# One core, a two-layer decoder trunk: the operand of the compression's first layer written position by position by engines, and fourteen weight pieces split by transfers

## The chip, the core and the metric

The kernel runs on one core of one Trainium2 chip. The core has five engines that run at the same time, each through its own list of instructions in order: TensorE (PE, matrix products; its weight loads are listed as PEld), VectorE (DVE), ScalarE (ACT), GpSimd (POOL) and SyncE (SP, which here only starts transfers). Transfers run on 16 DMA engines that all queues share. The metric is device time in microseconds (us) of one launch; three runs of the kernel before gave 584.83, 585.29 and 585.83 us, median 585.29.

## What is computed

The input is 256 tokens of width 1024, in float32. Layer 0 is a recurrent block (two input products, a convolution of width 4, gates, a scan, an output product) and a squared-ReLU MLP of width 4096. Layer 1 is sparse attention and a second MLP. The attention has 16 heads in four groups and three branches. The change lies in the first branch, which compresses keys and values:

```python
def _compress(z, pe, w1, w2):
    B, S, G, DH = z.shape                       # 1, 256, 4, 64
    n_chunk = S // CMP_STRIDE                   # 16
    nc = n_chunk - CMP_RATIO + 1                # 15
    chunks = z.reshape(B, n_chunk, CMP_STRIDE, G, DH)
    blocks = jnp.concatenate([chunks[:, r:r + nc] for r in range(CMP_RATIO)], axis=2)
    blocks = blocks + pe[None, None, :, None, :]
    flat = jnp.transpose(blocks, (0, 1, 3, 2, 4)).reshape(B, nc, G, CMP_LEN * DH)
    return jax.nn.gelu(flat @ w1, approximate=True) @ w2
```

So 15 overlapping blocks of 32 positions, for four groups, each of 32 x 64 numbers, go through a product with `w1` (2048 to 64), a gelu and a product with `w2`. This is done for keys and for values. `flat @ w1` is the first layer that the title speaks of.

## The kernel before

**Precision and pieces.** All large products are made from a high and a low part in the fast float32 format ("fp32r"): three products for one (lines 328, 329, 330 in `mm3`). A weight is stored as pieces of 128 x 1024 numbers, 512 KB, in the order in which they are used. A piece is brought to the array in one of two ways. Split by engines: SP loads it into one of five `raw` buffers (L274), ACT or DVE casts it to the high part in one of seven `whl` buffers (L288 or L336), DVE subtracts (L297 or L333) to get the low part. Split by transfers (`split_dma`): a transfer from POOL's queue loads it straight into the high buffer (L388, the target's type does the rounding), ACT or DVE writes the negated high part into the low buffer (L390), and a second transfer from POOL's queue adds the piece to that (L392). `BY_DMA` names the pieces that go the second way; before, these are eight of the fifteen pieces from q3 on.

**Stages.** By the trace PE's last product of layer 0's recurrent block starts at 89.6 us and layer 0's MLP ends at 263.8; the attention section's products run from there to 398.7, and the second MLP and the final norm end the program. In the MLPs the order is written out by hand. In the two other sections a planner (`Plan`) sets it: each operation is added with its engine or a choice of engines, an assumed duration, what it reads and writes, and a due time; random shifts from a list of seeds move the due times; a list schedule gives the start of each, and instructions are emitted in that order. Another list of seeds gives another order. Real waits are by semaphores, so the planned times only set the order on each engine.

**The attention section.** First come eight projections named by `EARLY` (ks0 kw0 q0 q1 ck0 ck1 cv0 cv1), then q2, the values (`v`, five pieces, L1019 to L1021), then q3, ks1, kw1 and q4 to q7 as fillers between the attention of the heads, and the output projection in two halves (o00 to o03, o10 to o13). Each head has its scores (L1149, L1150), a masked minimum on DVE (L1156), an exponential on ACT (L1159), a rescale on ACT or DVE (L1178), transposes on PE into banks 5 and 6 (L1189), copies of these as high part on ACT (L1192) and low part on DVE (L1193), and the product with the values (L1214, L1216).

**The compression.** `cproj` makes the projections ck and cv (two chunks each); after each, DVE multiplies by the norm (L943) into a buffer `tt` of 128 x 256. Four transfers of 64 x 240 numbers from SP's queue (L364, by `move`) then bring it into `zf`, the first layer's operand in the tile `zwoh`; there are sixteen in all. `zf` has 122 columns z (61 for keys and 61 for values: four groups of 15 blocks and one column of position codes) and 16 positions l in a block. `hidden` makes sixteen plain float32 matmuls (L957), one a position, 128 x 122 each: `e.matmul(hp(), w1[:, l], zf[:, :, l], ...)`. The planner takes 0.9 us for four of them. Before, the 16 positions of a column are neighbours in memory, so the 122 columns that one matmul reads lie 64 bytes apart. The two columns of position codes come by two small transfers from DRAM (L931). Behind `hidden` stands a chain of small operations: L963 (ACT, two copies), L965, L967, L968 (DVE), L969 (ACT), L970 and L971 (DVE), then the second layer on PE (L978 for keys, L997 for values).

Of the kernel before, what the change touches and what calls it, by code (L numbers as in the profile page):

```python
# [28 lines left out]
NB = 15  # L29
# [4 lines left out]
LATE = "q2 v q3 ks1 kw1 q4 q5 q6 q7".split()  # L34
TE = 2.73
W1T, T1, TH, TC, T2, T3, THS, THD, THT, NEARLY = -3.89, 3.12, 0.0, 4.6, 4.94, 3.03, 13.46, 6.73, 5.46, 8
SEEDS, ROUNDS, SHIFT, MOVES, SPREAD = ((3,), (144, 22097, 77409, 21939, 78114, 80006, 60630, 7069, 62773, 82469, 25830, 79801, 92020, 84794, 19920, 86923, 46302, 34626)), 6, 1.5, 12, 3.0
HPEN, LPEN, APEN, LEAD = 0.56, 1.0, 0.0, 9.0
RPEN = 0.51
WARM = 16  # L40
BY_DMA, DLEAD, NPEN = "q3 kw1 q5 q7 o01 o03 o11 o13", 8.0, 0.3
MLAG = (3.4, 4.0)
PLACED = "ks0 kw0 q0 q1 q2".split()
NI, NFINE = 3, 3
# [43 lines left out]
class Plan:  # L88
# [8 lines left out]
    def add(self, eng, dur, fn=None, r=(), w=(), t=0.0, lag=None):  # L97

        if fn is None:
            eng, fn = eng, dur  # L100
        if isinstance(eng, str):
            eng = [(eng, dur, 0.0)]
        i, deps = len(self.tasks), set()
        for k in r:
            if k in self.writer:
                deps.add(self.writer[k])
            self.readers.setdefault(k, []).append(i)
        for k in w:
            deps.update(self.readers.pop(k, ()))
            if k in self.writer:  # L110
                deps.add(self.writer[k])
            self.writer[k] = i
        deps.discard(i)
        self.tasks.append((eng, fn, sorted(deps), t, lag))
# [124 lines left out]
def trunk_kernel(ctx: ExitStack, tc: tile.TileContext, x_in, vec_in, const_in, w2_in, wts, out):  # L239
    nc = tc.nc  # L240
    ctx.enter_context(tc.manual_schedule())
    pe, dve, act, pool = nc.tensor, nc.vector, nc.scalar, nc.gpsimd
# [92 lines left out]
    def copy(o, a):  # L335
        return lambda e: (e.copy if e is act else e.tensor_copy)(o, a)  # L336

    zcols = lambda x: x[:, :S]
    HI = [("act", 0.31, 0.0), ("dve", 0.21, APEN)]
# [139 lines left out]
    vec = consts.tile([P, V_N], F32, name="vec")  # L479
# [55 lines left out]
    with ExitStack() as ph:  # L535
        rg = ph.enter_context(tc.tile_pool(name="rg", bufs=1))
        sec = Section()
        add, table = sec.add, sec.table
# [18 lines left out]
        for x in FIRST.split():  # L557
            n = 1 + x.endswith("+")
# [18 lines left out]
        for k in range(KC):  # L577
            g = vec[:, V_GM + k:V_GM + k + 1]
            t = 0.6 * k - 3
# [240 lines left out]
    with ExitStack() as ph:  # L820
# [96 lines left out]

        pre = ph.enter_context(tc.tile_pool(name="ct", bufs=1))
        ZW = 61
        zf = zw[0][:, :2 * ZW * 16].rearrange("p (z l) -> p z l", l=16)  # L920
        w1 = zw[1].rearrange("p (l c) -> p l c", l=16)
        zok, wok = [("oh", j) for j in range(8)], [("ol", j) for j in range(8)]
        cb = pre.tile([P, 1], F32, name="cb")
# [4 lines left out]
        bd = osumt.rearrange("p a (j e) -> p a j e", j=4)  # L928
        for i in range(2):
            pecol = (V_PEK, V_PEV)[i]  # L930
            add("sp", 0.5, lambda e, i=i, c=pecol: e.dma_start(zf[:, ZW * i + 60], vec_in[:, c:c + 16]), r=zok,  # L931
                w=[("z", i, "p")], t=W1T, lag=2.0)
            o, ws = offs[-1] + 4 * P * 1024, slice(8 * i, 8 * i + 8)
            add("sp", 1.5, lambda e, o=o, ws=ws: e.dma_start(w1[:, ws], wts[o:o + P * 2048].rearrange(
                "(p l c) -> p l c", p=P, l=16)[:, ws]), w=wok[4 * i:4 * i + 4] + ["loads"], t=W1T, lag=2.0)
        add("pool", 0.15, lambda e: e.memset(hid, 0.0), w=["hid"], t=-5)

        def cproj(i, gp, b, t, step):
            z, zk = proj_t(("ck", "cv")[i], gp, b, t, step)
            t += 4 * step  # L940
            n = ti["n"] = ti["n"] + 1
            x, xk = tt[n % 3], ("tt", n % 3)
            add("dve", 0.34, lambda e: e.tensor_tensor(x, z(), rs, op=OP.mult), r=[zk, "rs"], w=[xk], t=t)  # L943
            for hf in range(2):
                g = gp * 2 + hf
                for j in range(2):
                    dst = zf[own_(j), ZW * i + g * NB:ZW * i + (g + 1) * NB].rearrange("p n l -> p (n l)")
                    sec.move(dst, x[own_(hf), j * 16:j * 16 + 240], [xk] + zok, [("z", i, g, j)], t + 0.5, "sp")

        def hidden(b, t):  # L950
            hp = zview("hp", b, lambda x: x[:, :2 * ZW])
# [489 lines left out]
```

## Time and profile before

| what | number |
|---|---|
| median of three runs | 585.29 us (584.83 to 585.83) |
| the profiled execution | 585.05 us, its span 583.3 us |
| PE busy | 569.1 us, 98% of the span |
| PEld busy | 558.6 us, 96% |
| DVE busy | 418.3 us, 72% |
| ACT busy | 354.6 us, 61% |
| POOL busy | 56.3 us, 10% |
| DMA | 108.39 MB, 186 GB/s over the span |

Times in the trace count from the span's start. A PE row's duration runs from its start to its modelled end, and rows overlap; how fast PE really goes is read from start to start. "Idle before" names what ended an engine's wait. A row of 16 plain float32 matmuls of the program appears as 32 rows in the trace, two passes each. Line numbers of the changed kernel are one higher than before from line 947 on (L957 becomes L958, L1159 becomes L1160).

### The profile page before, as it was taken

The numbers are of one execution on the slowest core, as the hardware profiler recorded it, in microseconds if no ns is written. First come the engines' busy times: TensorE is split into PE (matmuls) and PEld (weight loads), VectorE is DVE, ScalarE is ACT, GpSimd is POOL, SyncE is SP. The second block draws the span as 40 slices with busy tenths as digits, with TensorE's granted clock in tenths as the row PEclk, the third lists the DMA queues.
The fourth block names the chain that finished last, engine by engine and source line by source line (L and its number), as shares of the span: only waits on it lengthen the run. The fifth ranks groups of instructions, "written<-read, shape, count | busy, mean of one in ns | idle before, by whom it ended". The sixth has DMA issues, their size and how long they took to land.

```text
span 583.3 us, 12179 instructions
## 1 busy us (share of the span) xinstructions
PE 569.1 (98%) x4756; PEld 558.6 (96%) x4756; DVE 418.3 (72%) x862; ACT 354.6 (61%) x712; POOL 56.3 (10%) x69
## 2 busy tenths in 40 slices
PE   8999999999999999999999989999999999999994
PEld 7999999999999999999999988989999999999994
DVE  6999998767665645647749989999866766464432
ACT  7699674856654433437628999986865664343410
POOL 1200000000000112211011100000000000132320
PEclk8999999999999999999999999999999999999998
DMA  8943575656556565566496776433666767467402
GB/s 286 389 127 136 182 229 197 222 188 199 195 186 213 184 217 177 189 222 217 107 332 173 157 185 172 140 70 109 227 212 183 199 198 241 156 185 219 139 2 72
DMA packets 34617, 108.39 MB, mean 186 GB/s; under 512 B 4576, under 2 KB 8304, under 8 KB 34560
## 3 DMA queue, kind: packets, MB, share of 16 engines
q1 hardware_dynamic: 31632, 98.61, 51.6%
q0 software_dynamic: 2352, 8.49, 6.5%
q8 instruction: 37, 0.61, 0.4%
q10 hardware_dynamic: 576, 0.53, 0.3%
q14 instruction: 20, 0.16, 0.1%
HBM read 103.48 MB, written 1.05 MB: 179 GB/s over the span
## 4 chain that ended last, share of the span: by engine, by line
PE 88%; ACT 5%; DVE 4%; DMA 1%; issue 0%; SPq 0%; DVEq 0%; ACTq 0%
PE bank L328 27%; PE bank L329 26%; PE bank L330 26%; PE bank L690 2%; ACT pt L1159 2%; PE bank L957 1%; ACT pt L1178 1%; DMA raw<-in_dram 1%; PE bank L1189 1%; DVE ptl L1193 1%; PE bank L1019 1%; ACT pth L1192 1%; PE bank L1021 1%; PE bank L1020 1%; DVE pt L1156 1%
## 5 line engine op out<-in xcount | busy, mean ns | idle before, releaser
L328 PE MATMUL bank<-hhl,whl 128*128 128x256 f32 x768 | 215.2, 280 | 1.5 <-DVE whl L336 1.2
L330 PE MATMUL bank<-hhl,whl 128*128 128x256 f32 x768 | 213.3, 278 | 0.2 <-DVE whl L333 0.2
L329 PE MATMUL bank<-hhl,whl 128*128 128x256 f32 x768 | 212.9, 277 | 0.0
L297 DVE TENSOR_TENSOR whl<-raw,whl 128x1024 fp32r<-128x1024 f32 x118 | 147.5, 1272 | 2.7 <-ACT whl L288 2.7
L328 PEld LDWEIGHTS bank<-hhl,whl 128*128 128x128 f32 x768 | 144.8, 189 | 2.4 <-ACT whl L336 1.4
L330 PEld LDWEIGHTS bank<-hhl,whl 128*128 128x128 f32 x768 | 144.7, 188 | 0.7 <-DVE whl L333 0.6
L329 PEld LDWEIGHTS bank<-hhl,whl 128*128 128x128 f32 x768 | 144.9, 189 | 0.2
L328 PE MATMUL bank<-uhl,whl 128*128 128x256 f32 x512 | 141.4, 276 | 0.0
L330 PE MATMUL bank<-uhl,whl 128*128 128x256 f32 x512 | 141.3, 276 | 0.0
L329 PE MATMUL bank<-uhl,whl 128*128 128x256 f32 x512 | 141.3, 276 | 0.0
L288 ACT CAST whl<-raw 128x1024 fp32r<-128x1024 f32 x119 | 121.3, 1043 | 23.0 <-issue 18.8
L328 PEld LDWEIGHTS bank<-uhl,whl 128*128 128x128 f32 x512 | 96.1, 188 | 0.0
L329 PEld LDWEIGHTS bank<-uhl,whl 128*128 128x128 f32 x512 | 96.1, 188 | 0.0
L330 PEld LDWEIGHTS bank<-uhl,whl 128*128 128x128 f32 x512 | 96.1, 188 | 0.0
L532 DVE TENSOR_TENSOR xt<-xt,bank 128x256 f32<-128x256 f32 x40 | 16.1, 418 | 84.4 <-PE bank L330 84.4
L333 DVE TENSOR_TENSOR whl<-raw,whl 128x1024 fp32r<-128x1024 f32 (+3 forms) x64 | 66.5, 1060 | 5.3 <-ACT whl L336 5.2
L785 ACT ACTIVATE u<-t 128x256 f32<-128x256 f32 x64 | 26.7, 417 | 56.1 <-DVE t L780 55.5
L336 ACT CAST whl<-raw 128x1024 fp32r<-128x1024 f32 (+3 forms) x54 | 50.4, 952 | 14.1 <-DMA raw<-in_dram 9.4
L780 DVE SCALAR_TENSOR_TENSOR t<-bank,rstd 128x256 f32<-128x256 f32 x64 | 26.9, 423 | 42.9 <-PE bank L330 42.4
L1317 ACT ACTIVATE xg<-xt,vec 128x256 f32<-128x256 f32 x8 | 4.1, 510 | 47.9 <-DVE xt L532 47.9
L1159 ACT ACTIVATE pt<-pt,mx 128x256 f32<-128x256 f32 (+1 forms) x64 | 28.6, 448 | 3.4 <-DVE mx L1156 3.3
L502 POOL TENSOR_TENSOR acc<-xt 128x256 f32<-128x256 f32 x2 | 3.0, 1521 | 266.0 <-DVE xt L532 266.0
(207 smaller groups left out, 822.8 us busy)
## 6 DMA issues: line engine op xcount, KB each, us to landing
raw<-in_dram SPq DMA_DIRECT2D x167, 512.0 KB, 4.0
whl<-in_dram POOLq DMA_DIRECT2D x16, 512.0 KB, 5.8
gw<-in_dram SPq DMA_DIRECT2D x4, 512.0 KB, 8.4
raw<-in_dram SPq DMA_DIRECT2D x6, 256.0 KB, 5.6
xt<-in_dram SPq DMA_DIRECT2D x4, 256.0 KB, 5.5
zwol<-in_dram SPq DMA_DIRECT2D x2, 512.0 KB, 5.5
zwoh<-tt SPq DMA_DIRECT2D x16, 60.0 KB, 2.7
raw<-in_dram SPq DMA_DIRECT2D x2, 456.0 KB, 5.3
```

The lines of the kernel that those rows point to most:

```text
L288: (act.copy if eng is None else eng.tensor_copy)(hi_t[i % NSPL][:, :n], raw_t[i % NRAW][:, :n])
L297: (eng or dve).tensor_tensor(lo[:, :n], raw_t[i % NRAW][:, :n], hi[:, :n].bitcast(F32), op=OP.subtract)
L328: pe.matmul(ps, wh, xh, start=start, stop=False)
L329: pe.matmul(ps, wh, xl, start=False, stop=False)
L330: pe.matmul(ps, wl, xh, start=False, stop=stop)
L333: return lambda e: e.tensor_tensor(o, a, h.bitcast(F32), op=OP.subtract)
L336: return lambda e: (e.copy if e is act else e.tensor_copy)(o, a)
L532: dve.tensor_tensor(xt[:, m], xt[:, m], z, op=OP.add)
L690: e.matmul(z(), gw[b][:, o:o + P], xb[2 * b + k], start=k == 0, stop=k == 1)
L780: dve.scalar_tensor_tensor(t, z, 0.0, rs, op0=OP.max, op1=OP.mult)
L785: act.activation(u, t, AF.Square)
L1159: add("act", (0.39, 0.49)[qc], lambda e, row=row, j=j: e.activation(row, row, AF.Exp, bias=mx[:, j:j + 1], scale=-1.0, accum_out=sm[:, j:j ...
```

## The change

`zf` is laid out position by position: the 122 columns of one position are neighbours, the 16 positions of a column lie 488 bytes apart. The sixteen transfers are replaced by sixteen copies of 64 x 240 numbers on ACT or DVE (`HI`, a choice that the planner makes), and the two small transfers by two POOL copies from `vec`, which is in SBUF since the program's start. `BY_DMA` holds fourteen pieces: q4, q6, o00, o02, o10 and o12 are added, so that from q3 on only ks1 is split by engines. And the seeds are others, so the planner's order of the attention section is another. The matmuls, their number and their shapes stay. The sections before and after keep their order.

```diff
@@ -34,11 +34,11 @@
-SEEDS, ROUNDS, SHIFT, MOVES, SPREAD = ((3,), (144, 22097, 77409, ..., 34626)), 6, 1.5, 12, 3.0
+SEEDS, ROUNDS, SHIFT, MOVES, SPREAD = ((3,), (123, 87858, 62944, ..., 89816)), 6, 1.5, 12, 3.0
...
-BY_DMA, DLEAD, NPEN = "q3 kw1 q5 q7 o01 o03 o11 o13", 8.0, 0.3
+BY_DMA, DLEAD, NPEN = "q3 q4 kw1 q5 q6 q7 o00 o01 o02 o03 o10 o11 o12 o13", 8.0, 0.3
@@ -917,7 +917,7 @@
-        zf = zw[0][:, :2 * ZW * 16].rearrange("p (z l) -> p z l", l=16)
+        zf = zw[0][:, :2 * ZW * 16].rearrange("p (l z) -> p z l", l=16)
@@ -928,8 +928,8 @@
         for i in range(2):
             pecol = (V_PEK, V_PEV)[i]
-            add("sp", 0.5, lambda e, i=i, c=pecol: e.dma_start(zf[:, ZW * i + 60], vec_in[:, c:c + 16]), r=zok,
-                w=[("z", i, "p")], t=W1T, lag=2.0)
+            add("pool", 0.15, lambda e, i=i, c=pecol: e.tensor_copy(zf[:, ZW * i + 60], vec[:, c:c + 16]), r=zok + ["vec"],
+                w=[("z", i, "p")], t=-5)
@@ -944,8 +944,9 @@
                 for j in range(2):
-                    dst = zf[own_(j), ZW * i + g * NB:ZW * i + (g + 1) * NB].rearrange("p n l -> p (n l)")
-                    sec.move(dst, x[own_(hf), j * 16:j * 16 + 240], [xk] + zok, [("z", i, g, j)], t + 0.5, "sp")
+                    dst = zf[own_(j), ZW * i + g * NB:ZW * i + (g + 1) * NB]
+                    y = x[own_(hf), j * 16:j * 16 + 240].rearrange("p (n l) -> p n l", l=16)
+                    add(HI, copy(dst, y), r=[xk] + zok, w=[("z", i, g, j)], t=t + 0.5)
```

How the order moves is shown at three places. First PE at the first layer of the compression. Before, where `whl,hhl` with 304 columns are the values:

```order
L1020 MATMUL bank_3612<-whl,hhl 128x304
L1021 MATMUL bank_3612<-whl,hhl 128x304
L957 MATMUL bank_3641<-zwoh,zwol 128x122 x16
L1019 MATMUL bank_3612<-whl,hhl 128x304
L1020 MATMUL bank_3612<-whl,hhl 128x304
```

Now, where bank_3557 is the projection q2:

```order
L329 MATMUL bank_3557<-hhl,whl 128x256
L330 MATMUL bank_3557<-hhl,whl 128x256
L958 MATMUL bank_3578<-zwoh,zwol 128x122 x16
L328 MATMUL bank_3557<-hhl,whl 128x256
L329 MATMUL bank_3557<-hhl,whl 128x256
```

The sixteen matmuls stood behind thirty matmuls of the values and now stand inside q2, before all of the values. Between the last matmul of cv1 and them stand 16 others (2 + 6 + 2 + 6: scores, q2, scores, q2).

Second DVE and ACT at the same place in the changed kernel. On DVE `tt_3215` and `tt_3216` are the two chunks of cv, and `zwoh` is the operand:

```order
L943 TENSOR_TENSOR tt_3215<-bank_3479,rstd 128x256
L336 COPY zwoh<-tt_3215 64x15x16 x3
L1157 ISA pt,mx_3238<-bank_3533,cst 128x256
L1157 ISA mx_3238 128x1
L1157 ISA pt,mx_3238<-bank_3533,cst 128x256
L1157 ISA mx_3238 128x1
L943 TENSOR_TENSOR tt_3216<-bank_3514,rstd 128x256
L336 COPY zwoh<-tt_3216 64x15x16 x3
```

On ACT, from the last copy to the gelu's part of the chain:

```order
L336 CAST whl<-raw_79 128x1024
L1160 ACTIVATE pt,sm_3242<-pt,mx_3238 128x256 x2
L336 COPY zwoh<-tt_3216 64x15x16
L1160 ACTIVATE pt,sm_3242<-pt,mx_3238 128x128 x2
L1160 ACTIVATE pt,sm_3243<-pt,mx_3239 128x128
L964 COPY cb<-bank_3578 64x1 x2
L390 ACTIVATE whl<-whl 128x1024
L970 ACTIVATE gy<-gy 128x60
```

Of the sixteen copies nine are on DVE and seven on ACT, and for the last chunk it is three and one. A negation of a piece that a transfer brings (L390) now stands between L964 and L970 on ACT. In all, DVE has six subtractions L333 of whole pieces fewer, two whole casts L336 fewer, two L390 more, and of the rescales (L1178) six with 256 columns and nine with 128 more, which ACT has fewer; ACT has four whole casts fewer and four L390 more, and four more casts of 64 or 128 x 256 that DVE gives up.

Third POOL's queue, which before had eight L388 and eight L392 and now has fourteen of each; the part behind the memory fills in the changed kernel:

```order
L388 DMA whl<-in_dram 128x1024
L392 DMA whl<-in_dram 128x1024
L388 DMA whl<-in_dram 128x1024 x3
L392 DMA whl<-in_dram 128x1024
L1054 COPY gcm<-gts 128x4x2 x4
L388 DMA whl<-in_dram 128x1024
L392 DMA whl<-in_dram 128x1024 x2
L388 DMA whl<-in_dram 128x1024 x2
L392 DMA whl<-in_dram 128x1024 x3
L388 DMA whl<-in_dram 128x1024 x3
L392 DMA whl<-in_dram 128x1024 x2
```

An L392 waits for the L390 of its piece, and what stands behind it on POOL waits with it. On SP's queue the sixteen moves are gone, and the loads of `raw` that stood behind them follow the loads that stood ahead of them; six loads of `raw` are gone too.

More of the change, by code (lines that the diff above doesn't have):

```diff
@@ L36 @@
 W1T, T1, TH, TC, T2, T3, THS, THD, THT, NEARLY = -3.89, 3.12, 0.0, 4.6, 4.94, 3.03, 13.46, 6.73, 5.46, 8
-SEEDS, ROUNDS, SHIFT, MOVES, SPREAD = ((3,), (144, 22097, 77409, 21939, 78114, 80006, 60630, 7069, 62773, 82469, 25830, 79801, 92020, 84794, 19920, 86923, 46302, 34626)), 6, 1.5, 12, 3.0
+SEEDS, ROUNDS, SHIFT, MOVES, SPREAD = ((3,), (123, 87858, 62944, 72224, 13667, 58707, 28766, 10748, 461, 68576, 75909, 30898, 22973, 69747, 33127, 16225, 86495, 85454, 50293, 89816)), 6, 1.5, 12, 3.0
 HPEN, LPEN, APEN, LEAD = 0.56, 1.0, 0.0, 9.0
```

## The prediction

> **What bounds the kernel now.** I read the page's busy times first, then the table of 40 slices, then windows of the attention section, then the waits of PE, and last single rows around the first layer of the compression. From the page's two first parts:
>
> ```profile
> PE 569.1 (98%) x4756; PEld 558.6 (96%) x4756; DVE 418.3 (72%) x862; ACT 354.6 (61%) x712; POOL 56.3 (10%) x69
> PE   8999999999999999999999989999999999999994
> DVE  6999998767665645647749989999866766464432
> ACT  7699674856654433437628999986865664343410
> PEclk8999999999999999999999999999999999999998
> ```
>
> PE is the bound nearly everywhere. The slices in which DVE and ACT are as full as PE are those of the attention section. Time can come from two sources there: PE work that gets shorter, and PE waits that go. The clock is full, so no time comes from it. Both MLPs and layer 0 keep their instructions and their order; I give them no term.
>
> The attention section by windows (busy of PE, PEld, DVE, ACT, POOL with instructions, then clock, DMA share, GB/s):
>
> ```profile
> 262.00:310.00 48.00, 47.68 (x372) 47.06 (x372) 32.77 (x84) 24.87 (x58) 6.26 (x13) 1.00 0.73 224
> 310.00:400.00 90.00, 86.74 (x659) 80.24 (x659) 84.98 (x320) 84.69 (x255) 8.01 (x11) 1.00 0.56 140
> PE bank L1189 <- DVE ptl L1193: 1.9, 2, 1.5
> PE bank L1189 <- ACT osum L1225: 0.4, 1, 0.4
> ```
>
> Up to 310 us DVE and ACT have 15 and 23 us to spare and PE waits 0.3 us. From 310 to 400 us all three are at 94% or more; PE idles 90 - 86.74 = 3.3 us, and the named waits are for DVE and ACT. Some waiting doesn't show as idle, because a row of PE lasts longer than its share:
>
> ```profile
> 360.59 0.39 PE L328 MATMUL bank<-oh,whl 128*128 128x256 f32 x1
> 361.05 0.39 PE L329 MATMUL bank<-ol,whl 128*128 128x256 f32 x1
> 361.28 0.28 PE L330 MATMUL bank<-oh,whl 128*128 128x256 f32 x1
> 306.03 0.28 PE L1020 MATMUL bank<-whl,hhl 128*128 128x256 f32 x1
> 306.15 0.28 PE L1021 MATMUL bank<-whl,hhl 128*128 128x256 f32 x1
> 306.54 0.41 PE L978 MATMUL bank<-hid,w2raw 128*128 128x64 f32 x2
> ```
>
> Undisturbed, the next matmul starts 0.12 us later (306.03, 306.15). Here 0.46, 0.23 and, ahead of L978, 0.39 pass. So beside the 3.3 us there may be as much again that no row calls idle.
>
> **Term A, the sixteen matmuls, -3.2 us.** The first layer and two other plain float32 products:
>
> ```profile
> 295.59 6.82 PE L957 MATMUL bank<-zwoh,zwol 128*128 128x122 f32 x32
> L957 PE MATMUL bank<-zwoh,zwol x32: 372/384/386, 295.6 to 302.0; 128*128 128x122 f32 x32
> 32.82 12.25 PE L690 MATMUL bank<-xb,gw 128*128 128x256 f32 x56
> L690 PE MATMUL bank<-xb,gw x64: 378/379/379, 28.3 to 44.7; 128*128 128x256 f32 x64
> 307.92 1.00 PE L997 MATMUL bank<-w2raw,pt 128*128 128x64 f32 x8
> ```
>
> From start to start L690 takes (12.25 - 0.379) / 55 = 0.216 us for 256 neighbouring columns; 122 columns at that rate are 0.103 us. L957 takes (6.82 - 0.384) / 31 = 0.208 us, twice that, with the same kind of weights; what differs is that its columns lie 64 bytes apart. The weight load sets no floor above this: the eight rows of L997, each with a load of the same size, take 1.00 / 8 = 0.125 us at the very most. In the new layout the columns are neighbours. I take 0.108, a little over the rate of L690, and 32 x (0.208 - 0.108) = 3.2 us. Bounds: 0 if the distance isn't the cause; 32 x 0.105 = 3.4 at L690's rate. PE has no idle time around these matmuls (47.68 of 48), so all of it counts.
>
> **Term B, the second layer's wait, -0.3 us.** PE lost 0.39 - 0.12 = 0.27 us ahead of L978. The chain that it waited for:
>
> ```profile
> 302.44 0.32 ACT L963 COPY cb<-bank 64x1 f32<-64x1 f32 x2 [5.15 <-PE bank L957]
> 304.44 1.23 DVE L333 TENSOR_TENSOR whl<-raw,whl 128x1024 fp32r<-128x1024 f32 x1 [0.44 <-ACT whl L336]
> 306.07 0.21 DVE L971 SCALAR_TENSOR_TENSOR hid<-gy,gx 128x60 f32<-128x60 f32 x1
> ```
>
> From 302.44 to 306.28 it took 3.8 us, of which a subtraction L333 of 1.23 us inside it. In the new order no L333 stands inside; without it and the waits around it I count about 2.2 us. PE now has 12 matmuls of q2 at 0.12 and 12 of the values at 0.14 between, 3.1 us. So the wait goes, with 0.9 us to spare. On ACT an L390 (1.06 us) now stands ahead of the chain's L969; it fits beside L965 to L968 if its transfer has landed, and costs PE what it is late by beyond 0.9 us. That risk is in term D.
>
> **Term C, DVE and ACT in the attention, -2.3 us.** Durations:
>
> ```profile
> L333 DVE TENSOR_TENSOR whl<-raw,whl 128x1024 fp32r<-128x1024 f32 x16 | 19.4, 1221 | 3.1 <-ACT whl L336 3.1
> L390 ACT ACTIVATE whl<-whl 128x1024 fp32r<-128x1024 f32 x5 | 5.3, 1057 | 0.5 <-DMA whl<-in_dram 0.5
> L336 ACT CAST whl<-raw 128x1024 fp32r<-128x1024 f32 x15 | 15.6, 1046 | 6.3 <-DMA raw<-in_dram 3.8 <-PE bank L329 1.7 <-ACT cb L963 0.6
> L1178 ACT ACTIVATE pt<-pt,sm 128x256 f32<-128x256 f32 x27 | 13.3, 503 | 0.8 <-DVE sm L1171 0.6
> L1178 ACT ACTIVATE pt<-pt,sm 128x128 f32<-128x128 f32 x29 | 10.9, 396 | 0.0
> L1178 DVE TENSOR_SCALAR pt<-pt,sm 128x256 f32<-128x256 f32 x5 | 1.6, 347 | 0.0
> L1178 DVE TENSOR_SCALAR pt<-pt,sm 128x128 f32<-128x128 f32 x3 | 0.8, 269 | 0.0
> L336 DVE CAST sb<-tt 64x256 fp32r<-64x256 f32 x1 | 0.3, 292 | 0.0
> ```
>
> The six added pieces save DVE 6 x 1.22 = 7.3 us of subtractions. Their casts (four ACT, two DVE) are replaced by as many negations at nearly the same price (1.057 for 1.046 on ACT). The rescales that move cost DVE 6 x 0.347 + 9 x 0.269 = 4.5 us and save ACT 6 x 0.503 + 9 x 0.396 = 6.6 us; four small casts move the other way, about 1.2 us off DVE and 1.6 onto ACT. Net: DVE 7.3 - 4.5 + 1.2 = 4.0 us less, ACT 6.6 - 1.6 = 5.0 us less, of 85 us each. The sixteen new copies are made before 295 us, where both have room: nine on DVE at 0.29 are 2.6 us, seven on ACT at about 0.4 are 2.8.
>
> What PE can gain is its waiting: 3.3 us that shows, at most as much again that doesn't. With DVE and ACT 5% emptier the waits won't all go, since some come from chains and not from load. I take 2.3 us, about a third of the upper end of 6.6; bounds 0 and 6.6. A new order alone could also bring waits; that is in the range.
>
> **Term D, waits for transfers, +0.4 us.** Six more pieces mean six more L390 that can stand at the head of ACT's or DVE's list until a transfer lands, and the exponentials, copies and subtractions behind them wait too, then PE. L390's waits for the transfer so far, and how long the issues take on POOL:
>
> ```profile
> DVE whl L390 <- DMA whl<-in_dram: 3.8, 1, 3.8
>   DMA whl<-in_dram: 5.0, 3
> L388 POOL DMA_DIRECT2D whl<-in_dram x8: 532/551/616, 289.0 to 362.4; - x8
> L392 POOL DMA_DIRECT2D whl<-in_dram x8: 868/883/945, 295.1 to 385.3; - x8
> ```
>
> Of eight L390 three waited, 5.0 us together, and 0.5 of it lay on ACT, where DVE's two fell into time with room (before 302.3). For PE none showed. I charge the six 0.07 us each, 0.4 in all. Bounds: 0, and 6 x 1.67 = 10.0 us if each waits as the three did and PE feels it.
>
> [...]
>
> **Term E, traffic, +0.3 us.** The six added adds (L392) move 3.1 MB more. The queues:
>
> ```profile
> q1 hardware_dynamic: 31632, 98.61, 51.6%
> q0 software_dynamic: 2352, 8.49, 6.5%
> DVE th L336 <- DMA sb<-th: 1.7, 1, 1.7
> ```
>
> SP's queue takes 51.6 / 98.61 = 0.52% of the span per MB. At that price the plain half of POOL's 8.49 MB takes 2.2%, so the adds take 4.3% for 4.2 MB, about 1% per MB: the six cost 3.1% of 583 us, 18 us of all DMA engines. From 310 to 400 us they are free for 44% of 90, 40 us. It fits, but small transfers land later in full stretches; one such wait (1.7 us on DVE, the cause of PE's longest, 1.5) is seen. I take a fifth of one more, 0.3; bounds -1.5 (counted in C) and +3.0 for two more.
>
> **Term F, nothing or nearly.** The moves leave SP's queue:
>
> ```profile
> 279.92 11.46 SPq L364 DMA_DIRECT2D zwoh<-tt  x16
> 296.24 1.05 ACT L336 CAST whl<-raw 128x1024 fp32r<-128x1024 f32 x1 [3.81 <-DMA raw<-in_dram]
> ```
>
> The loads behind them start up to 11 us earlier, and ACT's wait of 3.81 us goes. PE didn't feel that wait, covered by 30 matmuls of the values, so it gives 0. What comes in place of the moves is on the path: from the last matmul of cv1 to the sixteen stand 16 matmuls, 16 x 0.12 = 1.9 us. L943 (0.42) can start when that matmul's row ends, 0.28; three copies of 0.29 on DVE give 0.28 + 0.42 + 0.87 = 1.6 with some 0.1 for signals. No row shows an engine writing 488 bytes apart; at twice the price the copies are 1.74 and PE waits 0.6. Nearest is the 0.29 of the 64 x 256 cast; I take +0.1. [...]
>
> **The sum** is -3.2 - 0.3 - 2.3 + 0.4 + 0.3 + 0.1 = -5.0 us. On the profiled execution's 585.05 this gives 580.05, its span 578.3; that execution is 0.24 under the median, so 580.3 us for the runs. A change below 0.2% (1.2 us) can't be told from none.
>
> **The rivals.**
> 1. Only PE's own work shrinks; the waits between 310 and 400 come back in other places, because they are set by chains (scores, minimum, exponential, rescale, transpose) and not by load. For: PE's longest wait comes from a transfer, not from load. Against: DVE and ACT are at 94%. Time: 585.3 - 3.5 + 0.8 = 582.6. Chance 0.25.
> 2. The distance of columns isn't what makes L957 slow; the layout doesn't do what it says. For: only one line reads so. Against: the factor of two with like weights. The sum loses 3.2: 583.5. Chance 0.07.
> 3. Slower: late high parts stand at the head of ACT's and DVE's lists. Place: L390 between 310 and 390 us. Price 1.67 us each, 10.0 in all, against a gain of 5.4 without term D: 585.3 - 5.4 + 10.0 = 589.9. It decides from 0.9 us a piece on. Against: five L390 in the full stretch on ACT waited 0.5 us together. Chance 0.1.
>
> **How the numbers follow.** The forecast has 0.58, its own range 578 to 582. The 8-in-10 range reaches down to 576.5 (terms C near its upper end) and up to 583.8, which takes in the first two rivals. Faster by over 0.2%: nearly all of the forecast and rival 1, most of 2, 0.86. Within 0.2%: the edge of rivals 2 and 3, 0.06. Slower: rival 3 and bad luck of the order, 0.08.
>
> **What will show it.** A: L958's 32 rows within 3.4 to 3.8 us. B: no gap ahead of the second layer. C: DVE and ACT near 81 and 80 us in a stretch like 310 to 400, PE's idle there near 2 us or less. D: L390's waits for transfers of 1 us or less on ACT. E: DMA share near 0.7 there, no wait for `th` over 1.7 us. Wrong it would be if L958 stayed at 0.2 us a row, or if PE's waits for DVE and ACT grew past 4 us.

## The result, and the profile after

The forecast was wrong in its sign. The changed kernel takes 592.54 us (median of four runs, 591.97 to 593.55) against 585.56 of the kernel before in the same session (584.83 to 588.51): a ratio of 1.0116, 95% interval 1.0099 to 1.0134, so about 7 us slower. That is outside the range of 576.5 to 583.8. Of the kernels further down, one of ten executions of e2 and two of five of e8 ran in a slower state and are left out of their times.

The profiled execution took 592.92 us, its span 591.2; before it was 585.05 and 583.3. From the second part of the page, changed kernel:

```profile
PEclk9999999999999999999999889999999999999998
DMA  8943675666565665656379997602766666566401
```

In slices 23 and 24 of 40 (325 to 355 us) the granted clock is lower, and in slices 22 to 24 (310 to 355 us) the DMA engines are at nine tenths or more. So the first thing to look at is the stretch from 310 us on. The attention lies between the last product of the first MLP and the last product with `oh`. Rows of PE, first of the kernel before, then of the changed one:

```profile
263.76 0.28 PE L330 MATMUL bank<-uhl,whl 128*128 128x256 f32 x1
398.70 0.28 PE L330 MATMUL bank<-oh,whl 128*128 128x256 f32 x1
```

```profile
264.91 0.28 PE L330 MATMUL bank<-uhl,whl 128*128 128x256 f32 x1
405.29 0.28 PE L330 MATMUL bank<-oh,whl 128*128 128x256 f32 x1
```

Before it takes 134.9 us, now 140.4. Of the 7.9 us that the span grew, 5.4 are here, 1.2 ahead of it and 1.3 behind it. The windows of the changed kernel, the two of the prediction and then two of ten microseconds:

```profile
262.00:310.00 48.00, 47.04 (x387) 46.32 (x386) 40.19 (x109) 32.78 (x75) 8.04 (x16) 1.00 0.57 190
310.00:400.00 90.00, 82.18 (x600) 76.28 (x599) 72.58 (x290) 74.05 (x219) 16.43 (x22) 0.96 0.78 179
...
340.00:350.00 10.00, 7.85 (x68) 7.64 (x67) 7.46 (x23) 8.20 (x24) 3.75 (x5) 1.00 1.08 256
350.00:360.00 10.00, 9.13 (x56) 8.46 (x57) 6.67 (x32) 6.73 (x24) 1.43 (x2) 0.83 1.02 220
```

From 310 to 400 us PE now idles 7.8 us instead of 3.3, DVE and ACT are no longer full (72.6 and 74.1 us where it was 85.0 and 84.7), and the DMA share rose from 0.56 to 0.78, with stretches of ten microseconds at 1.02 and 1.08. So neither DVE nor ACT holds PE any longer, which the forecast wanted, and something else does. The waits of PE say what:

```profile
PE bank L1150 <- DMA sb<-tl: 3.0, 1, 3.0
PE bank L1087 <- DMA sa<-tl: 2.8, 1, 2.8
...
PE bank L958 <- DVE zwoh L336: 0.7, 1, 0.7
...
PE bank L524 <- DVE acc L467: 0.6, 1, 0.6
```

`sa` and `sb` are the operands of a head's scores: q3's and q4's rows, brought to their places by transfers of 64 KB from SP's queue (L364, by `move`). These transfers are not part of the change. Issues of such moves, the first of q3 and the two others of q4, and the PE rows that waited, changed kernel (SP's timeline, then PE's; L1087 is the score product with the compressed keys, L1150 that of a head):

```profile
321.54 0.59 SPq L364 DMA_DIRECT2D sa<-tl  x1
...
343.55 0.56 SPq L364 DMA_DIRECT2D sa<-tl  x1
344.16 0.59 SPq L364 DMA_DIRECT2D sb<-tl  x1
```

```profile
329.18 0.36 PE L1087 MATMUL bank<-kc,sa 128*128 128x32 f32 x2 [2.79 <-DMA sa<-tl]
...
350.87 0.55 PE L1150 MATMUL bank<-kh,sa 128*128 128x256 f32 x1 [3.02 <-DMA sb<-tl]
```

From the issue of q3's move at 321.54 to the row that waited for it 7.6 us pass. The second row waited for q4's moves; the profile names `sb<-tl`, the row itself reads `sa`, whose move was issued 7.3 us ahead of it. The table of DMA issues (target and source, how many, KB each, median us to landing) shows that this holds for the five pieces of q that are moved. First before, then the changed kernel:

```profile
sb<-tl SPq DMA_DIRECT2D x5, 64.0 KB, 3.6
sa<-tl SPq DMA_DIRECT2D x5, 64.0 KB, 4.0
```

```profile
sb<-tl SPq DMA_DIRECT2D x5, 64.0 KB, 6.7
sa<-tl SPq DMA_DIRECT2D x5, 64.0 KB, 6.4
```

Two and a half to three microseconds more to landing is as much as PE waits in each of the two places. The moves of k (`kh` and `kl`, of the same size) take 5.8 and 5.6 us in both kernels, so before, too, a move could take that long. What was in the queues then: POOL's own timeline, changed kernel.

```profile
310.55 0.55 POOL L388 DMA_DIRECT2D whl<-in_dram  x1 [1.12 <-PE bank L1022]
...
319.64 0.89 POOL L392 DMA_DIRECT2D whl<-in_dram  x1 [1.82 <-ACT whl L390]
...
340.14 0.88 POOL L392 DMA_DIRECT2D whl<-in_dram  x1 [1.78 <-ACT whl L390]
```

The first two are the first and the last of six transfers of 512 KB that start within 9 us, three of them adds (of q4, q5 and q6); the moves of q3 stand behind them. The third is the add of o01; with that of o02 at 342.47 and a load at 343.87 it stands ahead of q4's late moves.

The two waits are paid a second time. In the five microseconds up to the end of the second one PE was mostly idle; behind it, it ran without a gap at a lower granted clock (windows of five microseconds):

```profile
346.00:351.00 5.00, 1.98 (x17) 1.80 (x15) 2.59 (x7) 2.58 (x6) 1.44 (x2) 0.98 1.08 283
351.00:356.00 5.00, 5.00 (x24) 4.38 (x24) 2.69 (x13) 2.93 (x11) 0.89 (x1) 0.68 1.12 242
```

Two rows of the product with the values in that stretch, then two rows of the scores as wide, behind it, at a clock of 1.00 (355 to 360 us):

```profile
352.29 0.63 PE L1217 MATMUL bank<-pth,vhl 128*128 128x512 f32 x1
352.72 0.63 PE L1217 MATMUL bank<-ptl,vhl 128*128 128x512 f32 x1
...
355.38 0.40 PE L1150 MATMUL bank<-kh,sa 128*128 128x512 f32 x1
355.61 0.39 PE L1151 MATMUL bank<-kl,sa 128*128 128x512 f32 x1
```

From start to start a row of 512 columns takes 0.43 us there and 0.23 behind it. An estimate in proportion to the clock: five microseconds at 0.68 are worth 3.4 at 1.00, so this stretch costs 1.6 us; the ten from 330 to 340 behind the first wait, at 0.83, cost 1.7 in the same way. Together with the waits, 5.8 us, that is 9.1 us: more than the whole loss. The shorter matmuls give back a part of it.

### The profile page after: what moved, and what is told of

It is laid out like the page before. It is cut to its first block, busy times and chain, and to the rows that moved or that the text cites. A ratio compares the mean times of both kernels' runs of the same rounds, so it can differ in the third digit from the quotient of the medians.

```text
span 591.2 us, 12163 instructions
## 1 busy us (share of the span) xinstructions
PE 571.5 (97%) x4756; PEld 561.5 (95%) x4756; DVE 420.4 (71%) x876; ACT 357.9 (61%) x708; POOL 66.5 (11%) x83
## 4 chain that ended last, share of the span: by engine, by line
PE 74%; DVE 11%; ACT 6%; DMA 5%; issue 2%; POOL 1%; SPq 0%; DVEq 0%; POOLq 0%
PE bank L328 23%; PE bank L329 23%; PE bank L330 23%; DMA whl<-in_dram 3%; DVE whl L333 3%; ACT pt L1160 1%; PE bank L690 1%; DMA sb<-tl 1%; ACT pt L1179 1%; ACT pth L1193 1%; DVE t L722 1%; DMA raw<-in_dram 1%; PE bank L958 1%; ACT osum L1226 1%; DVE ptl L1194 1%
## 5 line engine op out<-in xcount | busy, mean ns | idle before, releaser
L333 DVE TENSOR_TENSOR whl<-raw,whl 128x1024 fp32r<-128x1024 f32 (+3 forms) x58 | 59.4, 1046 | 3.3 <-PE bank L330 2.2
L336 ACT CAST whl<-raw 128x1024 fp32r<-128x1024 f32 (+3 forms) x50 | 46.4, 946 | 9.6 <-DMA raw<-in_dram 5.7
L1160 ACT ACTIVATE pt<-pt,mx 128x128 f32<-128x128 f32 (+1 forms) x64 | 28.7, 449 | 8.3 <-DVE mx L1157 7.9
```

The costliest lines, as they stand in the source:

```text
L333: return lambda e: e.tensor_tensor(o, a, h.bitcast(F32), op=OP.subtract)
L1160: add("act", (0.39, 0.49)[qc], lambda e, row=row, j=j: e.activation(row, row, AF.Exp, bias=mx[:, j:j + 1], scale=-1.0, accum_out=sm[:, j:j ...
```

## The experiments

The theory from these rows: the adds' bytes delay the moves, and PE pays twice. The rivals: the issues on POOL (their number, a busy DVE beside them) and not the bytes; late high parts at the head of ACT's and DVE's lists (the prediction's third rival); the new order alone; the strided copies. Each comparison is with runs of the kernel before in the same session. Profiles of e3, e5 and e8 come from executions that were about 4 to 7 us longer than the median of their runs (that of e12 2.3), so only the waits that they name and single groups of rows are read.

### The adds' bytes: all of them, six, four late, four in the middle

**e1**, on the changed kernel. All fourteen adds move an eighth of their columns; orders and issues stay. The low parts are then incomplete.

```diff
-e.dma_start(lo, src, accum_op=OP.add)
+e.dma_start(lo[:, :128], src[:, :128], accum_op=OP.add)
```

> The changed kernel with every adding transfer (L392) cut from 1024 to 128 columns, all orders the same. Left out: the low part of seven eighths of each of the fourteen pieces holds the negated high part only. Theory 1 (traffic: the adds fill the DMA engines, so small moves and high parts land late): the moves' median landing falls from 6.2 us to 4 or less, PE's two waits for moves (3.0 and 2.8 us) and the two stretches at granted clock 0.83 that follow them go: 592.5 - 5.8 - 3 = about 583.5 us. Theory 2 (the new order itself, moves and chains stand badly, whatever the traffic): within 1.5 us of 592.5.

Measured: 582.78 us (582.39 to 589.04), before 585.78 in that session, ratio 0.9967 (0.9931 to 1.0002); 9.8 us less than the changed kernel. Moves and high parts in the table of issues, and the windows:

```profile
whl<-in_dram POOLq DMA_DIRECT2D x14, 512.0 KB, 4.9
...
sb<-tl SPq DMA_DIRECT2D x5, 64.0 KB, 4.9
sa<-tl SPq DMA_DIRECT2D x5, 64.0 KB, 3.2
```

```profile
310.00:400.00 90.00, 87.72 (x678) 82.22 (x676) 81.42 (x309) 82.09 (x237) 16.20 (x22) 1.00 0.50 122
```

The two waits for moves are gone but for 0.3 us, the clock stays at 1.00, and the attention takes 130.6 us, 9.8 less than in the changed kernel. POOL still makes 28 issues, of the same 0.55 and 0.89 us, so it is the bytes, not the issues. The waits, 5.5 us less, and the lower clock behind them, 3.3, make 8.8 of the 9.8 us. PE's idle in this window is 2.3 us, DVE is at 81.4 and ACT at 82.1: what the prediction expected of a good end ("near 81 and 80", "near 2 us or less"). It came about only without the traffic.

**e2**, the same for the six added pieces alone; **e14** for the four late ones (o10 to o13); **e15** for the four in the middle (q4 to q7).

```diff
-e.dma_start(lo, src, accum_op=OP.add)
+m = 128 if "%s%d" % order[i] in ("q4", "q6", "o00", "o02", "o10", "o12") else n
+e.dma_start(lo[:, :m], src[:, :m], accum_op=OP.add)
```

> The changed kernel with the adding transfer cut to 128 columns only for the six added pieces (their low parts are left incomplete), all orders the same. Theory 1 (traffic): with adds as many as before, at least two thirds of what the cut of all fourteen gives, about 586 us. Theory 2 (order): 592.5 within 1.5. If the high parts' loads and not the adds fill the engines: above 590 here, too.

> The changed kernel with the adding transfer cut to 128 columns for o10 to o13 only (low parts of these left incomplete), all orders the same. These four are the last of the fourteen in POOL's list. If what costs is an add next to small moves that PE waits for, these four are nearly free, because the moves are over by then: 590.5 to 592.5 us, PE's two waits for moves stay. If each add costs alike (9.8 / 14 = 0.7 us): 589.7.

> The changed kernel with the adding transfer cut to 128 columns for q4, q5, q6 and q7 only, all orders the same. These adds stand where q3 to q7, ks1 and kw1 are moved. If the place decides: most of the 9.8 us that the cut of all fourteen gave, 583.5 to 586.5, PE's waits for moves 1.5 us or less in all. If each add costs alike: 589.7.

Measured: e2 587.55 us (586.10 to 594.77), ratio 1.0039 (1.0007 to 1.0072), 5.0 less than the changed kernel, which is half of what e1 gives and not the two thirds that were expected. e14 594.38 (593.02 to 600.17), 1.0165 (1.0112 to 1.0219), no gain. e15 588.87 (587.90 to 596.02), 1.0076 (1.0043 to 1.0110), 3.7 less. PE's waits for moves, one fence each for e2, e14 and e15:

```profile
PE bank L1150 <- DMA sb<-tl: 1.9, 1, 1.9
...
PE bank L1087 <- DMA sa<-tl: 0.9, 1, 0.9
```

```profile
PE bank L1150 <- DMA sa<-th: 3.6, 1, 3.6
...
PE bank L1087 <- DMA sa<-tl: 3.1, 1, 3.1
```

```profile
PE bank L1150 <- DMA sb<-tl: 4.0, 1, 4.0
```

The late adds show no cost, though they are as large as the others; POOL issues the last four at 354 us or later, behind both long waits. So the place counts, not the megabytes alone. The time of e15 by itself doesn't say so: it lies near the 589.7 of "each add costs alike", not in the 583.5 to 586.5 of the other theory. Its waits do. The first wait went (0.4 us left), and the adds of q4 to q6, which stood ahead of it, are the ones that were cut. The second stayed at 4.0, and the adds of o01 and o02 ahead of it were left whole: 7.0 and 7.7 us to landing in e15, issued 4.2 and 1.9 us ahead of q4's move. In e2, where q4, q6 and o02 are cut but q5 and o01 are not, 0.9 and 1.9 us of the two waits stay. Cutting o01 and o02 by themselves was not tried.

### The same adds in the order of before

**e11**, on the kernel before: its eight adds cut as in e1. **e7**, on the kernel before: the six pieces added to `BY_DMA`, layout and seeds as they were (the planner then makes an order of its own).

```diff
-BY_DMA = "q3 kw1 q5 q7 o01 o03 o11 o13"
+BY_DMA = "q3 q4 kw1 q5 q6 q7 o00 o01 o02 o03 o10 o11 o12 o13"
```

> The kernel before with the adding transfers of its eight pieces cut to 128 columns (low parts left incomplete), all orders the same. Traffic theory: with eight adds the DMA engines are mostly not full, so this gives far less than the 9.8 us in the changed kernel: 0 to 2.5 us, 583 to 585.5. If each add costs alike wherever it stands (9.8 / 14 = 0.7 us): 5.6 us, 580.

> The kernel before (old layout, sixteen moves, old seeds) with the six pieces added to those split by transfers; the planner makes an own order. Traffic theory: slower than before by 4 to 8 us, 590 to 593, DMA share near 0.8 from 310 to 400 us, moves landing in 5.5 us or more at the median. If the added pieces are harmless and the new layout or the new seeds are to blame: 583 to 586.

Measured: e11 583.76 us (583.13 to 583.84) against 586.23, ratio 0.9943 (0.9922 to 0.9965); e7 596.63 (595.72 to 597.79) against 586.05, 1.0180 (1.0152 to 1.0207). The moves of e11, and PE's longest wait in e7:

```profile
sa<-tl SPq DMA_DIRECT2D x5, 64.0 KB, 2.4
```

```profile
PE bank L1086 <- DMA sa<-tl: 5.7, 2, 3.3
```

So even the eight adds before cost 2.5 us by the medians, though no wait of PE is named for a move: this move took 4.0 us where it could take 2.4, and PE's waits for DVE's low parts (L1189, 1.9 us before, the longest of which the prediction had traced to a late move) are 0.4 us in e11. Six more pieces split by transfers, with nothing else of the change but an order of its own, come out 10.6 us slower and bring the same wait for q's moved rows. This is the nearest to the change's second part alone; how much of it is the order isn't separated.

### The layout by itself

**e3**, the changed kernel with the old layout: the copies write neighbours, the matmuls read 64 bytes apart.

```diff
-zf = zw[0][:, :2 * ZW * 16].rearrange("p (l z) -> p z l", l=16)
+zf = zw[0][:, :2 * ZW * 16].rearrange("p (z l) -> p z l", l=16)
```

> The changed kernel with the operand's old layout (16 positions of a column are neighbours, 122 columns 64 bytes apart), still written by engines, all orders the same. If the matmul's gain is on the path: L958 at 0.208 us a row again, 3.0 us more, 595.5. If later waits for transfers take it up, since these come at fixed times after the issue of the moves: 592.5 to 593.5. The copies write neighbours here: if writing 488 bytes apart was dear, PE's wait of 0.7 us ahead of L958 goes.

Measured: 595.86 us (594.22 to 599.58), 1.0161 (1.0121 to 1.0201), 3.3 more than the changed kernel by the medians. PE's wait ahead of L958 is gone, as expected with cheaper copies. The sixteen matmuls of the changed kernel and of e3 (duration min/median/max in ns, first and last start):

```profile
L958 PE MATMUL bank<-zwoh,zwol x32: 275/275/343, 292.4 to 295.9; 128*128 128x122 f32 x32
```

```profile
L958 PE MATMUL bank<-zwoh,zwol x32: 384/384/428, 292.7 to 299.2; 128*128 128x122 f32 x32
```

(295.9 - 292.4) / 31 = 0.113 us a row against (299.2 - 292.7) / 31 = 0.210. The distance of the columns is the cause of the slow rows. The other side of it, the copies, in the changed kernel and in e3 (groups from 270 to 300 us):

```profile
L336 DVE COPY zwoh<-tt 64x240 f32<-64x240 f32 x9 | 5.4, 596 | 0.2
L336 ACT COPY zwoh<-tt 64x240 f32<-64x240 f32 x7 | 4.5, 640 | 0.2
```

```profile
L336 ACT COPY zwoh<-tt 64x240 f32<-64x240 f32 x7 | 2.7, 391 | 0.6 <-DVE tt L943 0.3
L336 DVE COPY zwoh<-tt 64x240 f32<-64x240 f32 x9 | 2.6, 289 | 0.2
```

Writing 488 bytes apart doubles DVE's price (596 ns for 289) and adds 64% to ACT's (640 for 391).

**e4**, the kernel before with one line changed: the matmuls read 122 neighbouring columns of `zwoh`, whatever stands there (so the compression's numbers are others). Transfers, order and all else stay.

```diff
-e.matmul(hp(), w1[:, l], zf[:, :, l], start=l == 0, stop=l == 15)
+e.matmul(hp(), w1[:, l], zw[0][:, l * 2 * ZW:(l + 1) * 2 * ZW], start=l == 0, stop=l == 15)
```

> The kernel before, all orders and transfers the same, only that the first layer's matmuls read 122 neighbouring columns of the operand's tile (the wrong ones: the compression's result is another). If the gain of the matmuls is on the path alone: L957 at 0.113 us a row or less and 585.4 - 3.0 = 582.4 us. If waits behind it take it up: 584.5 to 585.5.

Measured: 587.48 us (585.71 to 590.13), 1.0027 (1.0002 to 1.0052): no gain but a loss of 1.7 us, which neither of the two expectations had, though the 32 rows now run from 295.7 to 299.2 us, 0.113 each. PE's first wait, then DVE's timeline, both of e4:

```profile
PE bank L978 <- DVE gts L1028: 2.9, 1, 2.9
```

```profile
302.70 0.70 DVE L390 TENSOR_SCALAR whl<-whl 128x1024 fp32r<-128x1024 f32 x1 [4.36 <-DMA whl<-in_dram]
303.31 0.57 DVE L965 TENSOR_SCALAR gx<-bank,cb 64x60 f32<-64x60 f32 x2
```

The gelu's chain (L965), which ends in L978, stands on DVE behind an L390 that starts only at 302.70, after a wait for its high part, as it does before (there it starts at 302.31 after 3.76 us of wait). The matmuls were 3 us faster into a chain that couldn't start earlier, so PE waited 2.9 us ahead of the second layer (the profile names L1028, which stands on DVE directly behind the chain's last step L971). Behind this wait, too, the clock is lower: 0.83 on the mean from 300 to 310 us (0.96 from 262 to 310), where before it is 1.00; in proportion that is another 1.7 us. In the order of before, the first layer was not on the path alone: a transfer stood beside it, hidden behind the slow matmuls.

### Order and number of pieces

**e5**: the changed kernel with the eight pieces of before and the new seeds; **e6**: the same with the seeds of before. Layout and copies stay those of the change. **e8**: the changed kernel with a planner that is told longer transfers.

```diff
-BY_DMA = "q3 q4 kw1 q5 q6 q7 o00 o01 o02 o03 o10 o11 o12 o13"
+BY_DMA = "q3 kw1 q5 q7 o01 o03 o11 o13"        # e5; e6 also with the seeds of before
...
-MLAG = (3.4, 4.0)
+MLAG = (6.2, 6.2)                              # e8; and the lag of L388 7.1 for 4.8
```

> The changed kernel with the eight pieces of before split by transfers, new layout, engine copies and new seeds kept; the planner makes an own order from this. Traffic theory: the moves land in 4 us or less, PE waits for moves less than 1.5 us in all, 583 us (1 to 4 below the kernel before). If the new layout and the copies are worth nothing whatever the order, since later waits take the gain: 585 to 587.

> As the run with eight pieces, but with the seeds of before: new layout and engine copies alone, in an order of its own. Traffic theory: again 582 to 585, and no wait of PE for a move over 1.5 us. The distance between this run and the one with the new seeds is what an order is worth with the same work: I expect 1 to 3 us.

> The changed kernel with the planner told what the trace shows: moves land after 6.2 us (not 3.4) and high parts after 7.1 (not 4.8); the work is the same, the order another. If the loss is that the order counts on landings that the traffic delays, an order that allows for them gets most of it back: 584 to 588, PE's waits for moves under 2 us. If the engines of the transfers are simply full: 590 or more.

Measured: e5 591.45 us (588.69 to 597.41), 1.0094 (1.0065 to 1.0122); e6 585.69 (583.83 to 588.26), 0.9995 (0.9977 to 1.0013); e8 591.46 (589.44 to 591.77), 1.0080 (1.0050 to 1.0109). PE's longest wait in e5, in e6 and in e8:

```profile
PE bank L1087 <- DMA kl<-tl: 2.0, 1, 2.0
```

```profile
PE bank L1190 <- DVE ptl L1194: 3.6, 4, 2.3
```

```profile
PE bank L1190 <- DVE ptl L1194: 3.2, 4, 2.0
```

e5 and e6 do the same work with the same bytes, and their times differ by 5.8 us, where 1 to 3 had been expected. Both expectations for e5 (583, or 585 to 587) failed: with eight pieces, too, PE waits 3.2 us for moves in its order (2.0 and, for `sa`, 1.2). So a comparison of two orders that the planner made can be off by this much. In e8's profile the waits for moves are gone from the list, as was wanted, but waits for DVE's low parts of the transposes stand there instead, and by the medians 1.1 us were won, where an order that allows for the landings was to get most of the loss back.

### The new layout in the order of before

To keep the order out of the comparison, the last four kernels hold the order and the eight pieces of before, and put each copy where the move was issued, so that the order of everything else stays. The position columns come from POOL as in the change. They differ only in the engine of the sixteen copies: **e9** twelve on ACT and four on DVE, **e10** all on ACT, **e12** eight and eight, **e13** twelve on ACT and four on POOL.

```diff
-zf = zw[0][:, :2 * ZW * 16].rearrange("p (z l) -> p z l", l=16)
+zf = zw[0][:, :2 * ZW * 16].rearrange("p (l z) -> p z l", l=16)
...
-sec.move(dst, x[own_(hf), j * 16:j * 16 + 240], [xk] + zok, [("z", i, g, j)], t + 0.5, "sp")
+add("sp", 0.6, lambda e, f=copy(dst, y), h=dve if hf and j else act: f(h), ...)   # e9
```

> The kernel before with its own order and eight pieces kept, only the layout changed and the sixteen moves made into copies at the places where SP issued the moves (twelve on ACT, four on DVE), the position columns copied by POOL. If the layout and the copies are good in themselves and the loss came from the added pieces' traffic and the order: 582 to 583.5 us, since with the moves gone from SP's queue the loads come earlier and the DVE wait for a high part ahead of the gelu's chain shrinks. If that wait stays (as where only the reading was changed): 585 to 587, PE's wait at L978 again 2 us or more.

> As the run with the order of before and copies, with all sixteen copies on ACT: the same within 1 us, since ACT has 4.6 of 10 us free from 280 to 290 and 7.2 from 290 to 300.

> As the run with the order of before and copies, with eight copies on ACT and eight on DVE. With twelve on ACT, PE waited 1.2 us for the scores' minimum on DVE (L1156), which stood behind a subtraction that waited for a cast behind copies on ACT. With fewer copies on ACT that wait shrinks below 0.6 us: 582.5 to 583.5. If DVE's own copies delay it as much: 583.5 to 584.5.

> The order of before with layout and copies, twelve copies on ACT and four on POOL, which has room there. If the PE wait for L1156 comes from DVE's copy that stands ahead of it (0.6 us), it shrinks to 0.6 or less and the time is 583 us. If it comes from ACT's copies that hold up a cast (as with all copies on ACT, 1.9): it stays at 1.2 or more, 583.5 to 586.

| kernel | median us (range) | ratio (95%) | PE's wait at L1149 for L1156 | clock, 290 to 300 us |
|---|---|---|---|---|
| e9 | 583.73 (583.34 to 584.50) | 0.9948 (0.9930 to 0.9966) | 1.2 | 1.00 |
| e10 | 586.20 (585.17 to 588.53) | 0.9998 (0.9982 to 1.0014) | 1.9 | 0.83 |
| e12 | 585.67 (584.03 to 588.06) | 0.9999 (0.9983 to 1.0015) | 2.1 | 0.83 |
| e13 | 584.19 (583.53 to 586.32) | 0.9978 (0.9961 to 0.9995) | 0.5 | 1.00 |

The columns on the right come from rows like these, of e9 and then of e10:

```profile
290.00:300.00 10.00, 9.43 (x75) 9.46 (x76) 5.65 (x20) 5.79 (x17) 1.81 (x2) 1.00 0.76 268
```

```profile
PE bank L1149 <- DVE mx L1156: 1.9, 1, 1.9
...
290.00:300.00 10.00, 8.63 (x54) 8.66 (x55) 5.84 (x20) 8.13 (x21) 1.41 (x2) 0.83 0.62 217
```

So the layout with its copies, the sixteen moves gone, is worth 2.5 us where the copies fit beside the masked minimum's chain, and e9 beats both kernels. With four copies more (e10) or fewer (e12) on ACT the same matmul gain is spent: PE waits longer for the minimum (L1156), and from 290 to 300 us the clock is 0.83 instead of 1.00. Both were expected otherwise: e10 within 1 us of e9, e12 at 582.5 to 584.5. In e13 the wait shrank as expected, but not the time. That the longer wait comes from the copies' place in ACT's or DVE's list is the natural reading of four kernels that differ in nothing else; it is not shown, and which single copy it would be stays open. The wait of e4 is short in e9: with the sixteen moves gone from SP, the high part that L390 waits for comes sooner (2.33 us of wait on DVE instead of 4.36).

```profile
300.47 0.70 DVE L390 TENSOR_SCALAR whl<-whl 128x1024 fp32r<-128x1024 f32 x1 [2.33 <-DMA whl<-in_dram]
```

## Why the prediction was wrong, step by step

**Term E (traffic, +0.3) is the step that failed.** The prediction priced the six adds at 18 us of all DMA engines, set that against 40 us in which they are free between 310 and 400 us, and concluded "It fits". The price was near (POOL's queue rose from 6.5% to 11.0% of the span, which less the six added loads is about 17 us), and it does fit, on the mean: 0.78 in the window after. What failed is the step from the mean to the landing of a single move. In the changed order the adds and loads of the pieces come in groups of up to six, and where a group stood ahead of a move, the move came late. The moves of q took 6.4 to 6.7 us instead of 3.6 to 4.0, and in two places PE's next product needs them. The bytes of the fourteen adds cost 9.8 us in the changed order (e1), those of the six alone 5.0 (e2), those of eight in the old order 2.5 (e11). The upper bound of the term, +3.0 "for two more" waits, counted the waits rightly (there are two, of 2.8 and 3.0) but at half their length, and left out the lower clock behind them.

**Term C (DVE and ACT, -2.3) is not shown by any run.** With the adds' bytes cut on both sides, e1's attention takes 130.6 us, e11's 133.6 (from 263.80 to 397.43 us by the same two PE rows): 3.1 less, of which term A is 3.0 and the copies give back 0.7. So 3.1 - 3.0 + 0.7 = 0.8 us are left for terms B and C together. DVE and ACT did become emptier, as worked out; PE's idle from 310 to 400 us is 2.3 us in e1 and 1.8 in e11, so it isn't the emptier engines that lower it. This is near to rival 1. But the order differs between e1 and e11, and orders can make 5.8 us (e5, e6), so the 0.8 is no measurement of C.

**Term A (-3.2) was right on its rows and only half right on the path.** 0.113 us a row instead of 0.108, 3.0 us instead of 3.2; the medians of e3 and the changed kernel agree with it (3.3 us). Rival 2 falls. But "PE has no idle time around these matmuls, so all of it counts" isn't sound: e4 made the same rows as fast and won nothing, since the next thing on PE waited for a chain behind a transfer. What was needed is the slack of the next consumer, not PE's idle time beside the matmuls.

**Term B (-0.3)** held: no wait is named ahead of L979 in the changed kernel.

**Term D (waits for high parts, +0.4) was too small**, for the same cause as E: L390 waits 10.2 us in four places instead of 5.0 in three.

```profile
DVE whl L390 <- DMA whl<-in_dram: 5.5, 2, 3.3
ACT whl L390 <- DMA whl<-in_dram: 4.8, 2, 2.6
```

Rival 3 had charged the six pieces 10.0 us on top of the 5.0; the waits grew by 5.2. Its time, 589.9, is the nearest of all, but by number and not by mechanism: PE's two long waits end with the landing of a move, and it is the landing that came later. From q's scaling on DVE (L879) to the issue of its `sa` move it took 3.25 us for q3 and 3.11 for q4, in e1 2.97 and 2.96; from that issue to the landing 7.5 and 7.1 us, in e1 4.5 and 2.4. So from there on work queued behind late L390 put the moves back by 0.3 us at most. What the L390 waits cost elsewhere was not separated: every run that cut the adds shortened them too (2.9 us in e1), and 1.0 of e1's 9.8 us is left for that and all else.

**Term F (the copies, +0.1) was mis-sized.** Nearest had been taken the row of a copy to neighbours, 0.29 on DVE; measured are 0.60, and 0.64 on ACT for 0.4. The prediction's other bound, twice the price with 0.6 us of PE waiting, held: PE waits 0.7 us ahead of L958.

The issues on POOL beside a busy DVE don't explain the late landings: they take as long as before (L392 890 ns in the middle for 883), and in e1, with the same 28 issues, only small adds and a busier DVE (81.4 us from 310 to 400 for 72.6), the high parts land in 4.9 us in the median, as before, and not in 7.1.

```profile
L392 POOL DMA_DIRECT2D whl<-in_dram x14: 871/890/1014, 297.9 to 376.5; - x14
```

**What no step had.** The part behind the attention is 1.3 us longer, and a wait at the seam to the second MLP (L524 for `acc`, 0.6) is new; e1 and e5, with the new seeds, have it too (0.7), e6 and the kernels on the order of before don't. And "both MLPs and layer 0 keep their instructions and their order" is true, yet the part behind starts with a wait that the order ahead of it left. That the wait alone makes the 1.3 us was not shown. Of the 1.2 us ahead of the attention nothing is claimed: e1 shows 0.1 there with the same instructions.

**The sum again**, for the attention: before to e11, no adds' bytes, -1.3; e11 to e1, layout, relief and order, -3.1; e1 to the changed kernel, the bytes of fourteen adds, +9.8. That is +5.4, and with +1.2 ahead of it and +1.3 behind it the 7.9 us of the span. The kernel before paid for its eight adds already, so by this sum the change paid 9.8 - 1.3 = 8.5 us more for the bytes of adds (7.3 by the medians of e1 and e11), where term E has 0.3.

## What to carry to other kernels

Price a transfer by what else is in the queues when its result is needed, and look first for small transfers on the path that will share the engines with it; free DMA time on the mean did not tell their landing here. A gain on a full engine counts only as far as what that engine needs next can come sooner too: follow its next consumer, and ask which wait the slow work was hiding. When a change brings a new planned order with it, hold the order fixed and put the change into it (as in e9), or several microseconds of order will pass for the effect of the change.

## What the runs showed of the hardware

- Plain float32 matmuls with 122 moving columns take 0.113 us a row when the columns are neighbours and 0.208 to 0.210 when they lie 64 bytes apart (before, e3).
- Writes of one float each 488 bytes apart: a 64 x 240 copy takes 596 ns on DVE instead of 289 and 640 on ACT instead of 391.
- A move of 64 KB within SBUF (`sa<-tl`, median of five) took 2.4 us from issue to landing with the small adds of e11, 4.0 before and 6.4 in the changed kernel; a load of 512 KB from POOL's queue 4.9 us in the median before and in e1, and 7.1 in the changed kernel.
- Waits of 2.8 to 3.0 us of PE were followed by stretches at a granted clock of 0.68 over 5 us or 0.83 over 10 us, rows of 512 columns at 0.43 us instead of 0.23 (changed kernel, and 0.83 in e4); in proportion to the clock, an estimate, each such stretch cost 1.6 or 1.7 us beside the wait itself. In e10 and e12 the stretch from 290 to 300 us, with PE's wait at L1149 of 1.9 and 2.1 us in it, shows 0.83; in e9 and e13, where that wait is shorter, 1.00.
